# The conditioning matrix's middle part issued from POOL's DMA queue instead of SP's

## The chip, the cores and the metric

The kernel runs on one core of a Trainium2 chip. The metric is the device time of one execution, in microseconds (us). A kernel's time is the median of several executions. The trace comes from one more execution of the same program, taken by the hardware profiler; it has a time of its own, given below.

Engines: PE does matmuls and transposes, DVE and ACT work element by element, POOL and SP here do almost nothing but issue DMAs. A DMA issued by SP goes into SP's hardware queue, one issued by POOL into POOL's software queue; both queues are served by the same 16 DMA engines of the core.

## What is computed

One layer of a decoder trunk, batch 1, 512 tokens, width 2048. Six modulation vectors come from a conditioning vector; they scale, shift and gate the two halves of the layer.

```python
c_act = silu(c)
mod = c_act @ w_mod + b_mod                      # (2048) @ (2048, 12288)
sh1, sc1, g1, sh2, sc2, g2 = split(mod, 6)
h = rms_norm(x, norm_attn) * (1 + sc1) + sh1
qa, ka, va, qb, ckv, qi, ki, wi = split(h @ w_in)
out_a = swa_attention(qa, ka, va, ...)           # window 128, 16 heads
out_b = dsa_attention(qb, ckv, ..., qi, ki, wi)  # 128 keys per query chosen by an indexer, 16 heads
x = x + g1 * (concat(out_a, out_b) @ w_out)
h = rms_norm(x, norm_ffn) * (1 + sc2) + sh2
x = x + g2 * conv_ffn(h, w_up, conv_w, conv_b, w_down)
return rms_norm(x, norm_final)
```

The conditioning matrix w_mod is 2048 x 12288 float32, 100 MB. It is used once, against one vector.

## The kernel before

Float32 precision is kept by splitting every matmul operand in a high part (fp32r, a cast on ACT, line 129) and a low part (a subtraction on DVE, line 130), and by three matmuls per product (`mm3`, lines 134 to 136).

The program is a list of **slots**. A slot is a quarter of a projection unit: 256 KB of weights loaded by `load_raw` (line 123, tag `raw`, 7 buffers), split, and 12 matmuls of 128x512. `drive` walks the slots, loads five ahead and splits three ahead, and calls `step()` after each, which advances the generators that run beside the slots by one piece each. Those are the attention of a pair of heads (`pair_gen`), the preparation of keys and values for the next pair (`prep_gen`), and the conditioning matrix (`mod_gen`).

`mod_gen` goes through groups of 512 columns of w_mod. A group has 16 pieces of 128x512 (256 KB). Each piece is loaded, then multiplied by a column of the conditioning vector and added to `macc` on DVE (lines 181 and 183). After 16 pieces, 16 tiny matmuls (line 193) and one addition (line 230) give the group's columns of `mod`.

The stages, by the profile's time:

- 0 to 180 us: groups 0 to 7 with the keys and the indexer's queries.
- 180 to 390 us: heads of kind A, the indexer's selection (lines 601 to 649), and group 8.
- 390 to 626 us: heads of kind B, eight pairs, four slots a pair, with groups 9 to 13. Their pieces come through `ring_mod` (line 1196) into the ring `mrw` of 5 buffers, and 4 pieces are used per step. Every head also loads a bias tile `tbb` of 256 KB from a DRAM scratch (line 703); its source is a sliding view of one row, in two halves of 64 rows each (`toeplitz`, line 115).
- 626 to 812 us: the output projection `wo`, 64 slots, with groups 14 to 19. Their pieces come through `px_mod` (line 1238) into 8 buffers, 3 used per step. The residual `x` (four tiles of 1 MB, lines 1234 and 1246) is loaded in its first slots and stored again later (line 1265).
- from 812 us: the feed-forward, with groups 20 to 23 in its first part, again through `ring_mod`.

All of these loads are issued by SP, one after the other, in an order that a scheduler sets from priorities when the program is built. An instruction that waits holds back all that stand behind it in SP's order: a load waits for its buffer to be free (mostly for a DVE instruction), and sometimes for an earlier DMA that used the same semaphore. POOL's order is short in this part: three `affine_select` of the indexer (line 609), then nothing until the feed-forward's stores (lines 1064 and 1066).

Of the kernel before, what the change touches and what calls it, by code (L numbers as in the profile page):

```python
# [33 lines left out]
def hybrid_trunk(ctx, tc, xT, cT, wm, bm, nrm, wik, wiq, wi1, sinks, kvn, wuk, wuv, rel, onehot,  # L34
                 wo, wup, cw, cb, wdn, out):
    nc = tc.nc
    act, dve, pe, pool, sp = nc.scalar, nc.vector, nc.tensor, nc.gpsimd, nc.sync
# [80 lines left out]
    ki_ps = bank("acc", "ki_ps")  # L118


    def load_raw(src, name, tag="raw"):
        t = ring.tile([P, 512], F32, tag=tag, bufs=RING[tag], name=name)
        sp.dma_start(t, src)
        return t

    def split(raw, lo, n, name):
# [134 lines left out]
    class Raw:  # L261
# [3 lines left out]
        def load(self, part):  # L265
            if part not in self.t:
                self.t[part] = load_raw(self.src[:, 512 * part:512 * part + 512], f"{self.name}_{part}")
# [66 lines left out]
    with tc.tile_pool(name="ph0", bufs=1) as p0:  # L334
# [13 lines left out]
        def fetch_qi(j):  # L348
            src = wiq[j].rearrange("p a b -> p (a b)")
            for i in range(4):  # L350
                fetched["q", j, i] = load_raw(src[:, 512 * i:512 * i + 512], f"wiq{j}_{i}", "mrw" if i % 2 else "raw")
# [841 lines left out]


    def ring_mod(g, kt):
        return load_raw(wm[g, kt // 4][:, kt % 4], f"mraw{g}_{kt}", "mrw")

    start(ahead(index_gen(), 0))
    start(ahead(keys_gen(), 0))
# [3 lines left out]
    while idle:  # L1203
        step()
    start(mod_gen(range(8, 14), ring_mod, 5, p1, sc_ps, 4), low=True)
    drive(slots, marks["qb0"], marks["wo"])
    env["mh"] = mh = big.tile([P, KT, T], F32R, tag="b2", name="mh")
# [27 lines left out]

    def px_mod(g, kt):
        t = px.tile([P, 512], F32, tag="mraw", bufs=8, name=f"mraw{g}_{kt}")
        sp.dma_start(t, wm[g, kt // 4][:, kt % 4])
        return t

    start(mod_gen(range(14, 20), px_mod, 8, px, o_bank, 3), low=True)
    at = marks["wo"] + 6
    for i in range(1, 4):
# [23 lines left out]
    pdc = tc.tile_pool(name="ph4", bufs=1, reuse_waits="tile")  # L1267
    env["pd"] = pdc.__enter__()
    start(mod_gen(range(20, 24), ring_mod, 5, p2, o_bank, 2), low=True)
    drive(slots, marks["ff"] + 12, marks["join"])  # L1270
    pdc.__exit__(None, None, None)
# [95 lines left out]
```

## Time and profile before

| | |
|---|---|
| time, median of 3 runs | 2227.61 us (2227.18 to 2228.42) |
| time of the profiled execution | 2229.58 us |
| its span, first to last instruction | 2227.8 us |
| PE busy | 2149.5 us, 96% of the span |
| DVE / ACT / POOL busy | 1568.6 / 976.2 / 139.1 us |
| mean granted clock of PE | 0.985 |
| DMA | 367.09 MB, mean 165 GB/s |

The profiled execution lies 1.97 us above the median, and 1.78 us of it lie outside the span. "Busy" of an engine counts its instructions, not its waits. A releaser, shown after an arrow, is what ended an engine's idle time. The chain of waits is followed back from the last instruction, at each step to what released it. The granted clock is the mean of TensorE's two levels, 1.2 and 2.4 GHz, as a share of the upper one.

### The profile page before, as it was taken

Reading aid. Unit: us, or ns where it says so; the run is one execution under the profiler, and the core shown is the slowest. Engines: PE = TensorE matmul, PEld = TensorE weight load, DVE = VectorE, ACT = ScalarE, POOL = GpSimd, SP = SyncE. Lnnn points to the kernel's source line nnn. Section 1 sums busy time; section 2 is a strip of 40 time slices with the busy share of each in tenths; the row PEclk is TensorE's granted clock in tenths of the full one; section 3 lists DMA queues with packets and bytes.
Section 4 is the critical chain, followed back from the end, with each engine's and each line's share of the span. In section 5 each row is a group of like instructions: output and inputs, shape, how many; then the busy total and the mean of one; then the engine's idle time right before and its main releaser. Section 6 shows DMA issues by size and latency. Waiting matters only on the chain.

```text
span 2227.8 us, 30098 instructions
## 1 busy us (share of the span) xinstructions
PE 2149.5 (96%) x10376; PEld 1753.0 (79%) x10376; DVE 1568.6 (70%) x2829; ACT 976.2 (44%) x1850; POOL 139.1 (6%) x184
## 2 busy tenths in 40 slices
PE   7999999779889999999999999999999999999997
PEld 4777777667778888888888888888888888888887
DVE  3888999666679667875757576675757676675666
ACT  5334877556732254333333343333333343333332
POOL 0000000000000000000201011010201010010200
PEclk9999999989999999999999999999999999999998
DMA  9783422556489836743736565563737465563672
GB/s 395 258 292 105 114 72 69 172 172 190 134 301 330 286 99 215 251 150 113 161 101 161 122 135 141 133 149 111 162 98 163 121 136 143 131 150 111 116 256 76
DMA packets 181209, 367.09 MB, mean 165 GB/s; under 512 B 20159, under 2 KB 27343, under 8 KB 174912
## 3 DMA queue, kind: packets, MB, share of 16 engines
q1 hardware_dynamic: 157856, 321.15, 44.2%
q0 software_dynamic: 22336, 42.45, 12.9%
q8 instruction: 81, 1.33, 0.2%
q10 hardware_dynamic: 864, 1.57, 0.2%
q14 instruction: 72, 0.59, 0.1%
HBM read 312.93 MB, written 52.17 MB: 164 GB/s over the span
## 4 chain that ended last, share of the span: by engine, by line
PE 84%; DVE 6%; DMA 6%; ACT 3%; issue 1%; SPq 0%; DVEq 0%; ACTq 0%
PE p L1053 6%; PE p L1055 6%; PE p L1054 6%; DMA mraw<-in_wm_dram 4%; PE qip L134 1%; PE qip L135 1%; PE qip L136 1%; PE o L762 1%; PE tpb L748 1%; DVE macc L183 1%; PE mrow L188 1%; DVE wk L624 1%; DVE top L621 1%; PE mps L193 1%; DVE sa L726 1%
## 5 line engine op out<-in xcount | busy, mean ns | idle before, releaser
L169 ACT CAST dh<-rq 128x512 fp32r<-128x512 f32 x240 | 149.6, 623 | 182.7 <-PE p L1055 143.8
L183 DVE SCALAR_TENSOR_TENSOR macc<-mraw,cact,macc 128x512 f32<-128x512 f32 x240 | 179.7, 749 | 43.5 <-DMA mraw<-in_wm_dram 40.0
L170 DVE TENSOR_TENSOR dl<-rq,dh 128x512 fp32r<-128x512 f32 x240 | 160.9, 685 | 43.1 <-ACT dh L169 42.3
L1054 PE MATMUL p<-dl,ah 128*128 128x512 f32 x480 | 186.7, 389 | 0.0
L1053 PE MATMUL p<-dh,ah 128*128 128x512 f32 x480 | 186.7, 389 | 0.0
L1055 PE MATMUL p<-dh,al 128*128 128x512 f32 x480 | 186.7, 389 | 0.0
L1064 POOL DMA_DIRECT2D cd<-co x72 | 61.4, 852 | 875.1 <-DVE co L1077 873.8
L1054 PEld LDWEIGHTS p<-dl,ah 128*128 128x128 f32 x480 | 90.2, 188 | 18.7
L1053 PEld LDWEIGHTS p<-dh,ah 128*128 128x128 f32 x480 | 90.1, 188 | 18.8
L1055 PEld LDWEIGHTS p<-dh,al 128*128 128x128 f32 x480 | 90.0, 188 | 18.6
L1080 DVE TENSOR_TENSOR v<-p,v 128x512 f32<-128x512 f32 x120 | 82.3, 686 | 6.0 <-PE p L1055 5.2
L1064 POOL DMA_DIRECT2D cd<-v x72 | 61.4, 859 | 128.1 <-DVE v L1082 73.1
L170 DVE TENSOR_TENSOR al<-cu,ah 128x256 fp32r<-128x256 f32 (+2 forms) x60 | 46.7, 779 | 23.8 <-ACT ah L169 21.2
L169 ACT CAST ah<-cu 128x256 fp32r<-128x256 f32 (+2 forms) x60 | 41.5, 692 | 48.1 <-DVE cu L979 25.7
L1077 DVE TENSOR_TENSOR co<-p,v 128x512 f32<-128x512 f32 x80 | 54.9, 686 | 6.7 <-PE p L1055 6.7
L748 PE MATMUL tpb<-identr,sb 128*128 128x128 f32 x160 | 28.8, 316 | 26.0 <-ACT etb L749 26.0
L999 DVE TENSOR_TENSOR rq<-rq,rq 128x512 f32<-128x512 f32 x80 | 52.4, 684 | 0.0
L479 DVE TENSOR_TENSOR qi<-qi,qip 128x512 f32<-128x512 f32 x56 | 38.3, 684 | 14.4 <-PE qip L136 13.6
L748 PEld LDWEIGHTS tpb<-identr,sb 128*128 128x128 f32 x160 | 21.6, 161 | 33.7 <-ACT etb L749 29.6
L1066 POOL DMA_DIRECT2D cd<-co x8 | 4.4, 546 | 668.7 <-DVE co L1077 668.7
L170 DVE TENSOR_TENSOR dl_t<-tw,dh_t 128x512 fp32r<-128x512 f32 x40 | 27.7, 692 | 22.7 <-ACT dh_t L169 22.7
L728 ACT ACTIVATE sb<-sb,nmb 128x512 f32<-128x512 f32 (+2 forms) x64 | 35.3, 553 | 15.6 <-DVE nmb L726 15.3
(4496 smaller groups left out, 6431.2 us busy)
## 6 DMA issues: line engine op xcount, KB each, us to landing
mraw<-in_wm_dram SPq DMA_DIRECT2D x256, 256.0 KB
rq<-in_wdn_dram SPq DMA_DIRECT2D x160, 256.0 KB
mraw<-in_wm_dram SPq DMA_DIRECT2D x32, 1024.0 KB
cd<-co POOLq DMA_DIRECT2D x80, 256.0 KB, 4.5
cd<-v POOLq DMA_DIRECT2D x80, 256.0 KB, 4.7
wiq<-in_wiq_dram SPq DMA_DIRECT2D x32, 256.0 KB
wik<-in_wik_dram SPq DMA_DIRECT2D x8, 592.0 KB
xn<-in_xT_dram SPq DMA_DIRECT2D x4, 1024.0 KB
```

The costliest lines, as they stand in the source:

```text
L169: act.copy(hi_t, full)
L170: dve.tensor_tensor(lo_t, full, hi_t.bitcast(F32), OP.subtract)
L183: dve.scalar_tensor_tensor(acc, t, cact[:, kt:kt + 1], acc, OP.mult, OP.add)
L479: dve.tensor_tensor(qi[i], qi[i], ps, OP.add)
L748: pe.transpose(tp[:, i], self.s[:, c:c + P], ident)
L999: dve.tensor_tensor(self.b[out], self.b[a], self.b[b], OP.add)
L1053: pe.matmul(ps[b], ah[:, tok], wh, start=k == 0, stop=False)
L1054: pe.matmul(ps[b], ah[:, tok], wl, start=False, stop=False)
L1055: pe.matmul(ps[b], al[:, tok], wh, start=False, stop=k == 1)
L1064: pool.dma_start(cd[tb][dq], t, accum_op=OP.add)
L1077: dve.tensor_tensor(t, ps, box["v" if i == 1 else "u", b], OP.subtract)
L1080: dve.tensor_tensor(box["v", b], ps, box["v", b], OP.add)
```

## The change

`load_raw` gets the issuing engine as an argument. Groups 8 to 13 (through `ring_mod`) and groups 14 to 19 (through `px_mod`) are now issued by POOL, 192 loads of 256 KB in all; groups 20 to 23 stay on SP. Buffers, sizes and the arithmetic are as before.

```diff
-    def load_raw(src, name, tag="raw"):
+    def load_raw(src, name, tag="raw", by=sp):
         t = ring.tile([P, 512], F32, tag=tag, bufs=RING[tag], name=name)
-        sp.dma_start(t, src)
+        by.dma_start(t, src)
         return t
...
     def ring_mod(g, kt):
-        return load_raw(wm[g, kt // 4][:, kt % 4], f"mraw{g}_{kt}", "mrw")
+        return load_raw(wm[g, kt // 4][:, kt % 4], f"mraw{g}_{kt}", "mrw", pool if g < 14 else sp)
...
     def px_mod(g, kt):
         t = px.tile([P, 512], F32, tag="mraw", bufs=8, name=f"mraw{g}_{kt}")
-        sp.dma_start(t, wm[g, kt // 4][:, kt % 4])
+        pool.dma_start(t, wm[g, kt // 4][:, kt % 4])
         return t
```

The order of instructions moves as follows. SP, heads of kind B, at the loads of the fourth pair's weights (`qb4r`); `mraw` are pieces of the conditioning matrix, `tbb` the bias tiles, `wukr` weights of the key preparation:

```order
 L123 DMA qb4r_4290<-in_wi_dram 128x512
 L703 DMA tbb_4108<-biasd 128x1x512
-L123 DMA mraw_11_4016<-in_wm_dram 128x512
-L123 DMA mraw_12_4058<-in_wm_dram 128x512
-L123 DMA mraw_13_4061<-in_wm_dram 128x512
 L829 DMA wukr_4208<-in_wuk_dram 128x256
 L703 DMA tbb_4110<-biasd 128x1x512
-L123 DMA mraw_14_4064<-in_wm_dram 128x512
-L123 DMA mraw_15_4067<-in_wm_dram 128x512
-L123 DMA mraw_0_4112<-in_wm_dram 128x512
-L123 DMA mraw_1_4115<-in_wm_dram 128x512
 L123 DMA qb4r_4346<-in_wi_dram 128x512
```

On SP, bias tiles and weights are left, in their old order. POOL, around the indexer's three `affine_select`:

```order
+L123 DMA mraw_3_3860<-in_wm_dram 128x512
+L123 DMA mraw_4_3942<-in_wm_dram 128x512
 L609 AFFINE_SELECT isc_1630<-isc_1630 128x128
 L609 AFFINE_SELECT isc_1631<-isc_1631 128x128
 L609 AFFINE_SELECT isc_1632<-isc_1632 128x128
+L123 DMA mraw_5_3946<-in_wm_dram 128x512
+L123 DMA mraw_6_3949<-in_wm_dram 128x512
```

The fifth piece of group 9 (`mraw_4_3942`, the 21st load of the ring) now stands ahead of the selection in POOL's order, the sixth behind it. Up to the start of the output projection, the orders of PE, DVE and ACT are the same as before. From there on DVE's order changes; its first rows in the output projection (`wo2r` and so on are weights, `x_0` the residual, `macc_0_6151` the sum of group 14):

```order
 L130 TENSOR_TENSOR wo2r_2l<-wo2r_6031,wo2r_2h 128x512
+L181 TENSOR_SCALAR macc_0_6151<-mraw_0_6135,cact 128x512
+L183 SCALAR_TENSOR_TENSOR macc_0_6151<-mraw_1_6137,cact,macc_0_6151 128x512
+L183 SCALAR_TENSOR_TENSOR macc_0_6151<-mraw_2_6139,cact,macc_0_6151 128x512
 L908 SCALAR_TENSOR_TENSOR x_0_6112<-wo0ps,mod,x_0_6112 128x512
+L183 SCALAR_TENSOR_TENSOR macc_0_6151<-mraw_3_6141,cact,macc_0_6151 128x512
 L908 SCALAR_TENSOR_TENSOR x_0_6112<-wo1ps,mod,x_0_6112 128x512
-L181 TENSOR_SCALAR macc_0_6151<-mraw_0_6135,cact 128x512
+L183 SCALAR_TENSOR_TENSOR macc_0_6151<-mraw_4_6143,cact,macc_0_6151 128x512
 L130 TENSOR_TENSOR wo2r_3l<-wo2r_6117,wo2r_3h 128x512
```

The pieces are taken earlier: five stand ahead of the split of `wo2r_3` where one stood. Counted over the whole stage, the old order has 1 to 3 pieces per slot and once 11 (ahead of the split of `wo4r_1`); the new one has 1 to 5 everywhere, and both have used up their 96 pieces by the last slot of `wo11`. The stores of `x` (line 1265) move ahead on SP, from the start of the feed-forward into the loads of `wo6`, `wo10`, `wo14` and later.

## Rows read from the trace of the kernel before

**Rows 1.** The page, parts 1 and 4: PE's busy time; the chain's shares.

```profile
PE 2149.5 (96%) x10376; PEld 1753.0 (79%) x10376; DVE 1568.6 (70%) x2829; ACT 976.2 (44%) x1850; POOL 139.1 (6%) x184
...
PE 84%; DVE 6%; DMA 6%; ACT 3%; issue 1%; SPq 0%; DVEq 0%; ACTq 0%
PE p L1053 6%; PE p L1055 6%; PE p L1054 6%; DMA mraw<-in_wm_dram 4%; PE qip L134 1%; PE qip L135 1%; PE qip L136 1%; PE o L762 1%; PE tpb L748 1%; DVE macc L183 1%; PE mrow L188 1%; DVE wk L624 1%; DVE top L621 1%; PE mps L193 1%; DVE sa L726 1%
```

**Rows 2.** Busy time by stretch: six head pairs of kind B, then the rest.

```profile
core 0: us, PE busy (x) PEld busy (x) DVE busy (x) ACT busy (x) POOL busy (x), PEclk, DMA share, GB/s
396.30:430.50 34.20, 23.28 (x139) 19.20 (x137) 20.57 (x46) 18.02 (x44) 0.00 (x0) 0.85 0.53 168
430.50:464.30 33.80, 25.70 (x150) 20.78 (x150) 21.28 (x44) 17.39 (x42) 0.00 (x0) 0.85 0.58 174
464.30:494.80 30.50, 25.09 (x159) 21.19 (x158) 19.25 (x42) 18.94 (x45) 0.00 (x0) 0.94 0.52 154
494.80:522.40 27.60, 25.83 (x159) 21.04 (x158) 21.55 (x45) 18.52 (x44) 0.00 (x0) 0.94 0.71 214
522.40:552.40 30.00, 26.34 (x159) 21.67 (x158) 19.25 (x42) 18.72 (x45) 0.00 (x0) 0.89 0.56 171
552.40:582.60 30.20, 26.25 (x158) 20.66 (x158) 19.52 (x43) 19.31 (x46) 0.00 (x0) 0.94 0.57 180
582.60:626.00 43.40, 40.75 (x231) 33.48 (x231) 31.95 (x73) 36.57 (x87) 0.00 (x0) 0.92 0.48 147
```

**Rows 3.** The same view: the output projection's two parts, and heads of kind A.

```profile
626.00:752.00 126.00, 119.74 (x562) 96.84 (x562) 108.37 (x171) 32.65 (x56) 0.00 (x0) 0.99 0.94 324
752.00:812.00 60.00, 59.59 (x298) 50.21 (x297) 24.85 (x44) 17.64 (x28) 0.00 (x0) 1.00 0.53 178
240.00:300.00 60.00, 59.25 (x365) 48.04 (x364) 52.73 (x136) 54.41 (x147) 1.28 (x3) 1.00 0.34 95
```

**Rows 4.** Waits, 390 to 626 us: who waited for whom, us, times, longest.

```profile
DVE macc L183 <- DMA mraw<-in_wm_dram: 36.8, 12, 6.0
DVE macc L181 <- DMA mraw<-in_wm_dram: 2.0, 1, 2.0
PE tpb L748 <- ACT etb L749: 26.0, 6, 10.5
SPq L123 <- DVE macc L183: 42.0, 63, 3.8
```

**Rows 5.** SP's timeline: start, us, line, DMA, count.

```profile
472.67 0.51 SPq L703 DMA_DIRECT2D tbb<-biasd  x1
473.28 2.55 SPq L123 DMA_DIRECT2D mraw<-in_wm_dram  x4
```

**Rows 6.** The chain of waits in order of time: start, us, what.

```profile
473.28 9.48 DMA mraw<-in_wm_dram
```

**Rows 7.** DMA from 472 to 484 us in 40 slices: busy tenths, GB/s.

```profile
DMA  2114821295998889968989899998521111111111
GB/s 82 55 41 126 290 96 55 61 137 150 352 280 147 198 307 335 246 212 184 259 280 266 314 348 369 348 314 259 157 82 75 34 55 41 55 55 41 55 55 55
```

**Rows 8.** DMA issues from 396 to 582 us: count, size of one.

```profile
mraw<-in_wm_dram SPq DMA_DIRECT2D x76, 256.0 KB
tbb<-biasd SPq DMA_DIRECT2D x12, 256.0 KB
```

**Rows 9.** DMAs that POOL issues, lines 1066 and 1064: ns min/median/max; landing of L1066's.

```profile
L1066 POOL DMA_DIRECT2D cd<-co x8: 539/542/582, 919.7 to 977.4; - x8
DMA to landing us min/median/max: 2.2/3.0/6.8
...
L1064 POOL DMA_DIRECT2D cd<-v x72: 836/854/1145, 1068.5 to 2113.8; - x72
```

**Rows 10.** Timelines of SP and of POOL at the indexer's selection.

```profile
262.81 0.33 SPq L123 DMA_DIRECT2D mraw<-in_wm_dram  x1
...
290.33 0.29 POOL L609 TENSOR_SCALAR_AFFINE_SELECT isc<-isc 128x128 f32<-128x128 f32 x1 [189.42 <-DVE isc L601]
```

## The prediction

> **What bounds the kernel now.** I read the page first, then busy time by stretch, then the waits of the stretch that stood out, then the DMAs under them.
>
> PE is busy 96% of the span and makes 84% of the chain; the one foreign thing of size on the chain is the landing of `mraw`, pieces of the conditioning matrix, with 4% [rows 1]. Time can only come from where PE idles or runs at a lower clock. The stretches say where: with heads of kind A, PE is busy 59.25 of 60 us at clock 1.00; with heads of kind B the six pairs from 396.3 to 582.6 us take 27.6 to 34.2 us each, for about 25 us of PE work, at clocks from 0.85 to 0.94 [rows 2, 3]. PE idles 10.92 + 8.10 + 5.41 + 1.77 + 3.66 + 3.95 = 33.8 us there. DVE is busy 121 and ACT 111 of these 186 us, so neither is the bound.
>
> The waits name the cause. DVE, which works in order, stands still 36.8 us before line 183 (and 2.0 us before line 181) until a piece of `mraw` has landed, and PE's largest wait, 26.0 us before the transposes of `tpb`, lies behind that through DVE and ACT [rows 4]. The other pieces of matrix work do not wait so.
>
> Why does a piece land late? Take the longest case: SP issues a bias tile `tbb` at 472.67 and the next piece at 473.28, at once when its buffer came free [rows 5]; the piece lands 9.48 us later [rows 6]. The DMA engines are nearly all busy until about 480.5 us, and then for over 3 us only a tenth of them, at some 50 GB/s [rows 7]. The busy share of 0.1 to 0.2 is two engines of sixteen, so about 25 GB/s each: I read this as the bias tile, whose source has an outer dimension of two, going through two engines only, 128 KB each, some 5 us at 25 GB/s. Every piece of `mraw` issued behind it in the same queue has a sixteenth of its bytes behind it on those two engines. So the wait is for place in the queue, not for bandwidth: the DMA share is 0.52 to 0.71 in these pairs [rows 2]. SP's own waits (42.0 us for a buffer at line 123 [rows 4]) also hold back weights, but these are loaded five slots ahead.
>
> **The change, part by part.** *Issue.* 192 loads leave SP and come to POOL. POOL's plain DMAs of the same 256 KB took 0.54 us each [rows 9]; 192 of them are 104 us on an engine that has three instructions between 240 and 812 us. On the path each load costs at most 0.54 in place of the 0.33 us that SP takes [rows 9, 10].
>
> *Landing.* No row shows a load of this size from POOL. The nearest are POOL's plain stores beside the feed-forward's loads: 3.0 us from issue to landing, 2.2 to 6.8 [rows 9]. I take 3.0 for the loads, with 6.8 as the bad end. In the case above: free at 473.2, landed at about 473.2 + 0.54 + 3.0 = 476.8 us, and DVE had come to it at 482.8 - 6.0 = 476.8 us. The wait of 6.0 us would be gone. The ring has 5 buffers, and DVE takes bursts of up to six pieces at about 0.75 us, so the sixth arrives 0.54 + 3.0 us after the first is done, when 5 x 0.75 = 3.75 us have gone: no wait at the median, 3.6 us at the bad end.
>
> *What is late next.* The same two engines stay the tightest. A pair now loads 76/6.2 = 12.3 pieces and two bias tiles [rows 8], and four weight tiles and some 0.5 MB of smaller ones by the code. On each of the two engines that is 2 x 131 + 12.3 x 16.4 + 4 x 16.4 + 33 = 562 KB, or 22.5 us at 25 GB/s, against a PE floor of 24 to 25 us. So they are not the bound, but they have little room, and I leave 1.5 us of PE idle per pair. Bounds: 0 (as with heads of kind A), and 4 us if they run at 20 GB/s (28 us per pair).
>
> *Six pairs.* Idle: 33.8 - 6 x 1.5 = 24.8 us. Clock: busy time times what is missing to 1 gives 3.5 + 3.9 + 1.5 + 1.6 + 2.9 + 1.6 = 14.9 us [rows 2]. The fourth pair, with only 1.77 us idle, still ran at 0.94; if all stayed there, 14.9 - 9.3 = 5.6 us come back; if the pairs came to the clock of the row of heads A, all 14.9. I take 10.
>
> *The last stretch, 582.6 to 626 us.* Idle 2.65 us and 3.3 us of clock; its gap does not come from `mraw`. I take 1 us, of 0 to 5.9.
>
> *Output projection.* PE idles 6.26 us up to 752 us, the DMA share is 0.94 at 324 GB/s [rows 3]. The bytes stay the same, and 2 MB of stores of `x` come in from the feed-forward. 40 slots x 256 KB, 96 pieces, 4 MB of `x` and these stores are 41.7 MB; at 324/0.94 = 345 GB/s they need 121 us, less than the 126 that the part takes. Two full queues would get about 162 GB/s each, and a slot's weights need 256 KB per 2.7 us, 97 GB/s, so weights don't starve. The old order's lump of 11 pieces before one split, behind which PE waited, is gone; the new order asks for five pieces ahead of `wo2r_3`, which must land beside `x`. Between -5 and +6 us; I take a gain of 3.
>
> *POOL's order.* The three selections stand behind the 21st load. SP could issue that load at 262.81 us, and the selection starts at 290.33, when its scores are done [rows 10]: nothing, by 27 us of cover. From the feed-forward on nothing moves but four stores: nothing.
>
> Sum: 24.8 + 10 + 1 + 3 = 38.8 us. From the profiled execution's 2229.58 that is 2190.8; it lies 1.97 us above the median, so 2188.8, say **2189 us**.
>
> **A rule for it.** No row here shows two queues with loads on the same engines. The Trainium skill ("DMA: Bandwidth & Descriptors", section on queues, rings and completion order) states that each DMA engine goes round the queue rows that have work, one packet at a time; by that the pieces pass the bias tile at half rate, and the sum is the one above.
>
> **The rivals.**
>
> *All of it comes back* (0.06): 33.8 + 14.9 + 5.9 + 6.3 = 60.9 us, 2167 us. For it, PE's 98.8% with heads of kind A; against it, the two engines' load.
>
> *The two engines become the bound* (0.13). At 20 GB/s a pair takes 28 us: 6 x 3.05 = 18 us gained, and 4 elsewhere: 2206 us. For it: 562 KB per pair; against: 25 GB/s in [rows 7].
>
> *The change doesn't do what it says* (0.07). If an engine serves descriptors in the order of their issue whatever the queue, a piece still lands behind the bias tile. Then only SP's holds and the evened order count, 3 to 8 us: 2220 to 2225. Against it: POOL's stores landed in 3.0 us with SP's loads running.
>
> *Slower* (0.06): POOL issues too slowly. In the output projection 96 pieces have 126 us, 1.31 us each. Issues longer than that stretch the stage, and as DVE takes pieces in order, the weights' splits behind them, and so PE. The point from which it decides: the pairs gain 36 us, so (126 + 36)/96 = 1.7 us per issue makes the whole slower; at 2.0 us the stage takes 192 us, 66 longer, and the time is 2228 - 36 + 66 = 2258 us. Against it: 0.54 us, 0.85 for the accumulating stores, 1.145 at most [rows 9], with DVE busy beside them. The Trainium skill speaks for it ("SBUF — State Buffer", section on SBUF's two separate sides): a DVE operation that uses both ports locks POOL out of writing descriptors, and an issue of 0.62 us took 3.1 us beside such copies. By that figure, as an estimate, the stage would take 96 x 3.1 = 298 us. The rows of POOL's issues here don't agree with it: DVE's work in this kernel is nearly all subtractions and multiply-adds with two inputs.
>
> **How the numbers follow.** The forecast (2172 to 2202 us) has 0.68, all back 0.06, two engines 0.13, no effect 0.07, slower 0.06. The range from 2165 to 2212 takes in the first three, 0.87. A measurement of this kernel can tell 0.2%, 4.5 us, from no change: faster means under 2223. Of the no-effect case 0.04 lies under it and 0.03 above: faster 0.91, same 0.03, slower 0.06.
>
> **What would show it.** DVE's wait for `mraw` between 390 and 626 us falls from 38.8 us to under 10. The six pairs take about 25 us each, at clocks near 1, with a DMA share near 0.7. POOL's issues at lines 123 and 1238 take about 0.55 us. The part of the output projection with pieces takes 120 to 126 us. Nothing changes after it. It would be wrong if pieces from POOL land later than 5 us after issue, if PE finds another wait of 4 us per pair (bias tiles or weights late on SP), or if POOL's issues take over 1.3 us.

## The result and the profile after

| | before | after |
|---|---|---|
| time, median | 2227.39 us (2223.52 to 2228.42, 4 runs) | 2207.74 us (2204.59 to 2213.56, 4 runs) |
| ratio | | 0.9918, 95% interval 0.9893 to 0.9943 |
| the profiled execution: time, span | 2229.58, 2227.8 us | 2213.56, 2211.8 us |
| six head pairs, first to last | 186.3 us | 161.3 us |
| output projection, first matmul of `wo0` to that of `wo11` | 151.0 us | 155.8 us |

The kernel became 19.65 us faster by the medians; the forecast was 38.6. The profiled execution of after is the slowest of its four, 5.8 us above the median, so its stretches add up to less than the medians differ by (2229.58 - 2213.56 = 16.0 us).

By stretch, the first six cut at the same matmuls as the pairs of [rows 2]. The last three are cut only near those of [rows 2, 3] (PE executes 259 instructions in the seventh, 231 in before), so their lengths aren't compared here. The columns are stretch, its length, busy time of PE, PE's weight loads, DVE, ACT and POOL (instructions in brackets), granted clock, DMA share and GB/s.

```profile
400.80:427.20 26.40, 23.03 (x139) 19.34 (x138) 19.95 (x46) 17.95 (x44) 5.90 (x11) 0.94 0.63 212
427.20:453.70 26.50, 24.40 (x150) 19.92 (x150) 21.31 (x44) 17.30 (x42) 8.59 (x16) 0.94 0.63 199
453.70:478.40 24.70, 23.81 (x160) 19.82 (x158) 18.72 (x41) 18.65 (x44) 5.36 (x11) 1.00 0.64 204
478.40:504.00 25.60, 24.18 (x158) 19.73 (x158) 20.80 (x45) 18.32 (x43) 8.04 (x15) 1.00 0.72 224
504.00:531.20 27.20, 24.05 (x159) 19.71 (x158) 19.78 (x44) 18.37 (x44) 5.93 (x12) 1.00 0.61 196
531.20:562.10 30.90, 27.65 (x160) 21.73 (x158) 19.72 (x47) 19.57 (x46) 4.25 (x8) 0.89 0.60 192
562.10:607.00 44.90, 41.62 (x259) 33.95 (x260) 31.74 (x73) 37.79 (x89) 1.60 (x3) 0.96 0.53 166
607.00:736.00 129.00, 120.20 (x539) 97.82 (x536) 109.55 (x174) 31.45 (x53) 49.30 (x92) 0.95 0.93 331
736.00:796.00 60.00, 59.66 (x295) 50.22 (x293) 23.08 (x38) 17.74 (x28) 0.00 (x0) 1.00 0.38 125
```

The six pairs, the first six lines, gain 186.3 - 161.3 = 25.0 us. PE's idle time in them falls from 33.8 to 14.2 us (length minus PE busy, summed) and its busy time from 152.5 to 147.1, as the clock is higher. The first pair begins at 400.8 us instead of 396.3, so 4.5 us are lost ahead of it, and from `wo0` to `wo11` the output projection takes 155.8 us instead of 151.0. The pairs gain what was to be gained only in part (25.0 of 34.8 us), and two places that were costed at nothing or better cost time.

The waits from 390 us to the end of heads of kind B (607 us), with us in total, times and the longest:

```profile
POOL mraw L1238 <- DVE nmb L726: 53.7, 2, 27.7
DVE macc L183 <- DMA mraw<-in_wm_dram: 19.4, 17, 3.0
PE tpb L748 <- ACT etb L749: 9.1, 6, 3.4
```

DVE waits for pieces of the conditioning matrix 19.4 us instead of 38.8 [rows 4], in 17 waits of at most 3.0 us; PE's wait behind it falls from 26.0 to 9.1. POOL's 53.7 us are harmless: it waits for memory that the heads still hold, with nothing else to do.

POOL's part in the page of after, groups of instructions (busy us, mean ns | idle before) and DMA issues (KB each, median us to landing):

```profile
L123 POOL DMA_DIRECT2D mraw<-in_wm_dram x96 | 51.6, 538 | 357.6 <-DVE macc L181 131.1
L1238 POOL DMA_DIRECT2D mraw<-in_wm_dram x96 | 51.4, 536 | 133.4 <-DVE nmb L726 53.7
mraw<-in_wm_dram POOLq DMA_DIRECT2D x192, 256.0 KB, 5.6
```

An issue costs the 0.54 us of [rows 9]. A landing costs 5.6 us, not the 3.0 that I had taken from POOL's stores. The profile counts a landing from the start of the instruction that issues it, so the 0.54 us are part of the 5.6.

The chain of waits of after around one late piece (start us, us, what), and the timeline of SP at that place:

```profile
429.05 7.96 DMA mraw<-in_wm_dram
437.01 0.03 issue
437.03 0.02 DVEq L183
437.06 0.04 issue
437.10 0.75 DVE macc L183
```

```profile
427.53 0.51 SPq L703 DMA_DIRECT2D tbb<-biasd  x1
```

This is the case of [rows 5, 6] again, with the piece now in another queue. SP issues a bias tile at 427.53, POOL a piece at 429.05, and the piece takes 7.96 us where it took 9.48. DVE stands still for it once more, for 1.6 us instead of 6.0.

### The profile page after: what moved, and what is told of

Read it like the earlier page. It is cut to its first block, busy times and chain, and to the rows that moved or that the text cites. A ratio compares the mean times of both kernels' runs of the same rounds, so it can differ in the third digit from the quotient of the medians.

```text
span 2211.8 us, 30173 instructions
## 1 busy us (share of the span) xinstructions
PE 2149.8 (97%) x10376; PEld 1752.7 (79%) x10376; DVE 1567.8 (71%) x2829; ACT 975.8 (44%) x1850; POOL 242.2 (11%) x376
## 4 chain that ended last, share of the span: by engine, by line
PE 72%; issue 17%; DMA 5%; POOL 2%; DVE 2%; ACT 1%; SPq 0%; POOLq 0%; DVEq 0%; ACTq 0%
PE p L1053 6%; PE p L1055 6%; PE p L1054 6%; DMA mraw<-in_wm_dram 4%; POOL mraw L1238 1%; POOL mraw L123 1%; PE qip L134 1%; PE mrow L188 1%; PE qip L135 1%; PE qip L136 1%; DMA xn<-in_xT_dram 0%; DVE macc L183 0%; PE mps L193 0%; DMA wiq<-in_wiq_dram 0%; PE cT L1105 0%
## 5 line engine op out<-in xcount | busy, mean ns | idle before, releaser
L183 DVE SCALAR_TENSOR_TENSOR macc<-mraw,cact,macc 128x512 f32<-128x512 f32 x240 | 179.6, 748 | 26.2 <-DMA mraw<-in_wm_dram 22.5
L123 POOL DMA_DIRECT2D mraw<-in_wm_dram x96 | 51.6, 538 | 357.6 <-DVE macc L181 131.1
L1238 POOL DMA_DIRECT2D mraw<-in_wm_dram x96 | 51.4, 536 | 133.4 <-DVE nmb L726 53.7
L169 ACT CAST ah<-cu 128x256 fp32r<-128x256 f32 (+2 forms) x60 | 41.5, 692 | 49.4 <-DVE cu L979 25.9
L728 ACT ACTIVATE sb<-sb,nmb 128x512 f32<-128x512 f32 (+2 forms) x64 | 35.3, 552 | 13.3 <-DVE nmb L726 13.0
L378 DVE SCALAR_TENSOR_TENSOR macc<-mraw,cact,macc 128x512 f32<-128x512 f32 x54 | 40.3, 746 | 0.4
```

The source lines that it names most:

```text
L123: by.dma_start(t, src)
L169: act.copy(hi_t, full)
L183: dve.scalar_tensor_tensor(acc, t, cact[:, kt:kt + 1], acc, OP.mult, OP.add)
L1238: pool.dma_start(t, wm[g, kt // 4][:, kt % 4])
```

## The experiments

All eight are edits of the kernel before or after, each timed beside the kernel before on the same chip: e1 to e4 on one chip, e5 to e9 on another. The wait is DVE's for pieces of `mraw` (lines 181 and 183), from 390 us to the first matmul of the output projection; the pairs are the six of [rows 2]. The kernel before had medians of 2227.39, 2227.12 and 2226.62 us beside them.

| kernel | groups 8 to 13 | groups 14 to 19 | bias tile: engines, queue | DVE's wait, us | pairs, us | time, us | ratio (95%) |
|---|---|---|---|---|---|---|---|
| before | SP | SP | 2, SP | 38.4 | 186.3 | 2227 | 1 |
| after | POOL | POOL | 2, SP | 16.9 | 161.3 | 2207.74 | 0.9918 (0.9893 to 0.9943) |
| e1_ring_only | POOL | SP | 2, SP | 16.7 | 159.5 | 2201.22 | 0.9885 (0.9864 to 0.9907) |
| e2_px_only | SP | POOL | 2, SP | 38.8 | 185.6 | 2231.21 | 1.0016 (1.0004 to 1.0028) |
| e5_bias_by_pool | SP | SP | 2, POOL | 16.3 | 159.1 | 2204.29 | 0.9896 (0.9878 to 0.9913) |
| e9_bias4 | SP | SP | 4, SP | 18.5 | 163.8 | 2202.86 | 0.9891 (0.9876 to 0.9906) |
| e3_bias16 | SP | SP | 16, SP | 4.6 | 144.8 | 2187.14 | 0.9817 (0.9798 to 0.9837) |
| e7_bias16_ring | POOL | SP | 16, SP | 10.8 | 149.1 | 2192.49 | 0.9841 (0.9824 to 0.9857) |
| e8_bias16_px | SP | POOL | 16, SP | 5.6 | 145.7 | 2192.69 | 0.9841 (0.9823 to 0.986) |
| e4_bias16_pool | POOL | POOL | 16, SP | 11.0 | 149.6 | 2195.66 | 0.9856 (0.9835 to 0.9878) |

The theory after the result: pieces were late for their place behind the bias tiles in SP's queue; POOL's queue takes them out of that place, but they share the tile's two engines still, and land later than I had put in. The main rivals: SP's own waits for buffers hold the pieces (then the bias tiles don't matter), or engines serve in order of issue whatever the queue (then POOL's queue doesn't matter).

### Each half of the change alone

**e1_ring_only** leaves groups 14 to 19 on SP:

```diff
-        pool.dma_start(t, wm[g, kt // 4][:, kt % 4])
+        sp.dma_start(t, wm[g, kt // 4][:, kt % 4])
```

> The change for groups 8 to 13 alone (pieces of the ring issued by POOL); groups 14 to 19 stay on SP, and the orders of PE, DVE and ACT are those of the kernel before. Theory (the changed kernel gained 25 us in the head pairs and gave back some 5 us in the output projection because DVE's order and the residual's loads changed there): the pairs keep 24 to 27 us of gain, the output projection takes 151 us as before, and the time is 2200 to 2205 us. Rival (the loss in the output projection comes from the pairs ending earlier, whatever issues groups 14 to 19): the output projection takes 155 us or more, and the time is 2206 to 2210 us.

**e2_px_only** leaves groups 8 to 13 on SP:

```diff
-        return load_raw(wm[g, kt // 4][:, kt % 4], f"mraw{g}_{kt}", "mrw", pool if g < 14 else sp)
+        return load_raw(wm[g, kt // 4][:, kt % 4], f"mraw{g}_{kt}", "mrw")
```

> The change for groups 14 to 19 alone; groups 8 to 13 stay on SP, with the orders of PE, DVE and ACT of the changed kernel. Theory: no gain in the pairs (DVE waits 35 us or more for pieces), 3 to 6 us lost in the output projection: 2229 to 2234 us. Rival (the output projection is served as well from POOL, and its loss in the changed kernel has another cause): 2222 to 2228 us.

Measured: 2201.22 and 2231.21 us, both inside their theory's range. The whole gain, 25.9 us, is in the ring of groups 8 to 13; groups 14 to 19 on POOL cost 4.1 us by themselves, and the full change lies 6.5 us above the half. The same sign stands in both pairs with 16 engines: e8 above e3 by 5.5, e4 above e7 by 3.2 us, though there the intervals overlap.

Where e2 loses its time is not what was expected. In its trace the output projection takes 150.3 us from `wo0` to `wo11`, no more than the 151.0 of before, and not 3 to 6 us more; what that execution is behind, it loses ahead of the pairs, where the clock fell (see below). So the price of groups 14 to 19 shows in the medians, but its place isn't shown by e2.

### The bias tiles spread over the engines

**e3_bias16** is the kernel before, all pieces on SP. The scratch that the bias tiles are read from holds 16 shifted copies of each row instead of 2, so the outer dimension of a tile's source is 16:

```diff
-    biasd = dram.tile([32, 2, 1024], F32, name="biasd")
+    biasd = dram.tile([32, 16, 1024], F32, name="biasd")
...
-        return bass.AP(tensor=biasd.tensor, offset=biasd.offset + 2048 * (HEADS * g + head) + 384 * g + P - 1,
-                       ap=[[1024 - 64, 2], [-1, 64], [1, n]])
+        return bass.AP(tensor=biasd.tensor, offset=biasd.offset + 16384 * (HEADS * g + head) + 384 * g + P - 1,
+                       ap=[[1024 - 8, 16], [-1, 8], [1, n]])
...
-                for k in range(2):
+                for k in range(16):
```

> All loads on SP, as in the kernel before; only the bias tiles' source is laid out in 16 shifted copies in place of 2 (its outer dimension is 16 in place of 2), so that a tile should go through 16 DMA engines in place of two. The orders of PE, DVE, ACT and SP are those before. Theory (pieces landed late because they stood behind a bias tile on two engines): DVE's wait for pieces between 390 and 626 us falls from 38.8 us to under 15, PE gets 20 us or more back there, 2198 to 2208 us. Rival (SP's order holds the pieces back, or the landing is late for all loads): the wait stays at 30 us or more, and the time is 2222 to 2230 us.

**e4_bias16_pool** is the same edit on the kernel after.

> The changed kernel with the bias tiles' source in 16 copies, as in the run with that alone. Theory (POOL's pieces still land in 5.3 us at the median because bias tiles fill two engines): landing falls to 3 to 4 us, DVE's wait for pieces from 19 us to under 8, the pairs gain 6 to 10 us more, 2196 to 2202 us. Rival (5.3 us is what a load from POOL takes here): landing stays above 5 us, and the time is that of the changed kernel, 2204 to 2210 us.

Measured: 2187.14 and 2195.66 us. e3 gains 40.0 us without moving a load to another queue, about the forecast's sum for the change under study and 11 us more than the best that its theory allowed; its wait of 4.6 us lies far under the 15. In e4 neither side had it right: pieces land in 4.7 us, not in 3 to 4 and not above 5, and the wait is 11.0 us, not under 8, while the time is at the edge of the theory's range. The waits of e3 from 390 to 555 us:

```profile
PE tpb L748 <- ACT etb L749: 3.0, 5, 1.9
DVE macc L183 <- DMA mraw<-in_wm_dram: 4.6, 8, 1.3
```

and its DMA issues from 396 to 560 us (count, KB, median us to landing), then the shortest, median and longest landing of a piece from 396 to 541 us:

```profile
mraw<-in_wm_dram SPq DMA_DIRECT2D x74, 256.0 KB, 4.5
tbb<-biasd SPq DMA_DIRECT2D x14, 256.0 KB, 4.0
...
DMA to landing us min/median/max: 3.1/4.5/5.8
```

A bias tile now lands in 4.0 us, and a piece in 4.5, at most 5.8. SP still waits 37.5 us for `macc` in that window, against 38.5 in before from 390 us to its first matmul of the output projection: SP's waits for buffers are not what made the pieces late. That rival falls, and the two engines of the bias tile stand as the cause. The Trainium skill states the rule behind it ("DMA: Bandwidth & Descriptors", section "Why a DMA increments its semaphore by 16 and not by 1"): a copy is split over as many engines as the largest number up to 16 that divides the slowest dimensions of its two sides. The traces agree: with 2 in the outer dimension a piece behind the tile took 9.48 us, with 16 no piece of that window took more than 5.8.

One path of the delay isn't told apart. In before SP also stood still until earlier loads had landed:

```profile
SPq L123 <- DMA mraw<-in_wm_dram: 25.0, 8, 5.6
SPq L123 <- DMA tbb<-biasd: 7.2, 3, 3.0
SPq L829 <- DMA tbb<-biasd: 6.3, 2, 3.2
```

These 38.5 us come from the late landings, and in e3 1.5 us are left of them. No run shows how much of DVE's wait went through them and how much through the place on the two engines; both go with the tile's two engines.

In e3 the six pairs run at clock 1.00; three of their lines:

```profile
419.70:443.20 23.50, 23.12 (x150) 18.68 (x150) 21.19 (x44) 17.23 (x42) 0.00 (x0) 1.00 0.70 218
443.20:467.20 24.00, 23.80 (x159) 19.82 (x158) 18.91 (x41) 18.65 (x44) 0.00 (x0) 1.00 0.71 217
467.20:491.90 24.70, 24.40 (x159) 19.70 (x158) 21.49 (x47) 18.21 (x44) 0.00 (x0) 1.00 0.79 242
```

With POOL on top (e4), 8.5 us of the gain are lost again.

**e9_bias4** takes 4 copies instead of 16:

```diff
+    biasd = dram.tile([32, 4, 1024], F32, name="biasd")
...
+        return bass.AP(tensor=biasd.tensor, offset=biasd.offset + 4096 * (HEADS * g + head) + 384 * g + P - 1,
+                       ap=[[1024 - 32, 4], [-1, 32], [1, n]])
...
+                for k in range(4):
```

> All pieces on SP as before, the source of the bias tiles in 4 shifted copies instead of 2 (or 16), so that a tile goes through 4 DMA engines. Theory of the queue: a tile's landing halves from 9.48 us to about 5 us, the pieces behind it land some 4 us earlier, DVE's waits for pieces in the six pairs are 10 to 20 us (38.8 with two, 4.6 with sixteen) and the time is 2190 to 2207. Rival, a threshold: the pieces are late only while a tile takes longer than the ring of five hides, so 4 engines give all that 16 give, 2185 to 2190.

Measured: a wait of 18.5 us and 2202.86 us. That is between 2 and 16 engines, in the upper part of what the theory of the queue gave; there is no threshold by which four would do. With 2, 4 and 16 engines the wait is 38.4, 18.5 and 4.6 us. The trace doesn't name a packet's engine; that the number of engines is what counts is read from this row. (The 9.48 us that this expectation and that of e5 give to the tile are the landing of the piece behind it; how long the tile itself took with two or four engines, the traces don't tell.) Four engines instead of two gain about what POOL's queue gains (24 us against 26 in e1).

### The tiles moved instead of the pieces

**e5_bias_by_pool** is the kernel before with the bias tiles, still through two engines, issued by POOL:

```diff
-            sp.dma_start(self.tb[:, :self.nt], self.tb_src)
+            pool.dma_start(self.tb[:, :self.nt], self.tb_src)
```

> The kernel before, with one line changed: the two bias tiles of a head (tba, tbb, still through two DMA engines each) are issued by POOL, and every piece of the conditioning matrix stays on SP; the orders of PE, DVE and ACT are those of before. Theory of the place in the queue: a piece that SP issues is no longer behind a bias tile of its own queue, so it lands in 3.5 to 5 us, DVE's waits for pieces in the six pairs fall from 38.8 us to under 10, and the time is 2188 to 2205 (PE may wait for a tile where POOL's landing is later than SP's 9.48 us). Rival, the two engines: fourteen sixteenths of a piece go through free engines but the piece is complete only when its share in the two loaded engines is through, whatever queue asked for it, so the waits stay over 20 us and the time is 2208 to 2225.

Measured: 2204.29 us, inside the range of the theory of the place, but with a wait of 16.3 us where it said under 10. It hardly matters which of the two leaves SP's queue: the time is that of e1 within the intervals, and the wait is 16.3 us against 16.7. What is left is shown by the issues of e5 from 396 to 560 us:

```profile
mraw<-in_wm_dram SPq DMA_DIRECT2D x77, 256.0 KB, 5.6
tbb<-biasd POOLq DMA_DIRECT2D x13, 256.0 KB, 11.3
```

Pieces from SP take 5.6 us here too, against 4.5 with the tile spread. I read this so: in two queues a piece no longer waits for the whole tile, but it shares its two engines with it. So both rivals hold in part. Taking the tile out of the pieces' queue removes the larger part of DVE's wait (38.4 to 16.3 us), and spreading it removes a rest that a second queue can't (16.3 to 4.6). The tile's 11.3 us can't be put down to the sharing alone: POOL also cuts it into other packets (7474 under 512 B in this window, 1670 in before), and its landing from SP in before isn't in the trace.

### POOL's own price

**e7_bias16_ring** is e3 with groups 8 to 13 on POOL, **e8_bias16_px** e3 with groups 14 to 19 on POOL; with e3 and e4 they make a square. The one line of each:

```diff
+        return load_raw(wm[g, kt // 4][:, kt % 4], f"mraw{g}_{kt}", "mrw", pool if g < 14 else sp)
```

```diff
+        pool.dma_start(t, wm[g, kt // 4][:, kt % 4])
```

> Groups 8 to 13 of the conditioning matrix are issued by POOL, groups 14 to 19 by SP, and the bias tiles go through 16 DMA engines as in the best kernel so far (2187.1 us, which has all of this on SP). The orders of PE, DVE and ACT are the same as there. Theory: POOL's load takes its 5.3 us to land by itself, so DVE's waits for pieces are about 11 us in the six pairs against 4.6, and the time is 2188 to 2193. Rival: the 5.3 us come from the bias tiles' two engines, and with 16 engines POOL's pieces land in about 3.6 us; waits under 6 us, time 2184 to 2188.

> Groups 14 to 19 of the conditioning matrix are issued by POOL, groups 8 to 13 by SP, and the bias tiles go through 16 DMA engines. With the kernels that have both parts on SP (2187.1), both on POOL (2195.7) and the ring alone on POOL, this makes a square of four. Theory: the price of the second part on POOL is its own and has nothing to do with the bias tiles: 2190 to 2194, that is 3 to 7 us above both on SP; the clock falls again near 211 us, as in the three kernels so far with this part on POOL, although nothing of it has run by then. Rival: the price of both parts is one of the two sharing POOL's queue: then this kernel is at 2186 to 2189, and no fall of the clock near 211 us would say that the fall is a matter of the execution.

Measured: 2192.49 us with a wait of 10.8, and 2192.69 with a wait of 5.6. The issues of e7 from 396 to 560 us:

```profile
mraw<-in_wm_dram POOLq DMA_DIRECT2D x74, 256.0 KB, 4.6
tbb<-biasd SPq DMA_DIRECT2D x14, 256.0 KB, 4.2
```

A median landing of 4.6 us is neither the 5.3 of the theory nor the 3.6 of the rival, and it is what SP's pieces take in e3 (4.5). So the median isn't POOL's own: the bias tile's two engines add 0.9 (5.5 in after, over the same window). Still, POOL's wait is 6.2 us longer than SP's and the pairs 4.3 us longer, and e4 against e8 says the same (3.9 us). Two things differ in the traces. The longest landing is 7.3 us in e7 and 5.8 in e3. And POOL issues back to back every 0.79 us, as here in after:

```profile
429.05 0.54 POOL L123 DMA_DIRECT2D mraw<-in_wm_dram  x1 [0.25 <-DVE denb L738]
429.84 0.54 POOL L123 DMA_DIRECT2D mraw<-in_wm_dram  x1 [0.25 <-DVE macc L183]
```

SP does it every 0.64 us (in before at 489.19 and 489.83), and DVE takes a piece about every 0.78 us in its bursts (three in 2.33 us, at 428.79 in after). That these two make the 6.2 us wasn't tested. The ratios of e7 and e3 differ by 0.0024, with intervals that overlap; the pairs and the waits carry the reading more than the times do.

The price of groups 14 to 19 on POOL shows without any bias tile in two engines too (e8 above e3), as the theory had it; the intervals of these two overlap, so it is likely and not shown.

## Why the prediction was right and wrong

**The cause, right.** The bias tiles ahead of them make the pieces late (e3), and a second queue takes them out of that place (e1, e5). The case "no effect" falls by the same runs, and "slower" by the issue of 0.54 us.

**The landing, mis-sized.** This is the term that failed. I took 3.0 us from POOL's 16 plain stores beside the feed-forward, a stretch with less traffic, and kept 6.8 as the bad end; it was 5.5. By the prediction's own reckoning, the sixth piece of a burst is needed 3.75 us after the first buffer comes free. (The reckoning counts the issue twice: a landing is counted from the start of the issue, so 0.54 doesn't come on top, neither here nor in the 476.8 us of the case.) A landing of 5.5 leaves a wait of 5.5 - 3.75 = 1.8 us a burst where I had none; measured were 17 waits of up to 3.0. With 4.5 us, in e3, it would leave 0.8, and the eight waits measured there are at most 1.3. The trace of before gives no landing for any load of this stretch. But it has POOL's 144 accumulating stores of the same size, of which I had used the time to issue and not the landing:

```profile
L1064 POOL DMA_DIRECT2D cd<-v x72: 836/854/1145, 1068.5 to 2113.8; - x72
DMA to landing us min/median/max: 3.8/4.7/12.3
```

The prediction said that it would be wrong if pieces landed later than 5 us after issue, and so it came.

**Where the rest went.** Of the 38.8 us summed up, the profiled execution has 16.0. The six pairs are 9.8 us short (25.0 of 34.8), the output projection 7.8 (-4.8 in place of +3), and 4.5 were lost ahead of the pairs, where nothing was put in.

**The six pairs.** Idle was to fall by 24.8 us and fell by 33.8 - 14.2 = 19.6; busy time was to fall by 10 with the clock and fell by 5.4. Both are short for one reason, the waits that stayed: with nearly all of them gone in e3, idle is 3.8 us, the clock 1.00, and busy time falls by 152.5 - 141.0 = 11.5. So the 10 us for the clock was right in size, but not a term of its own; it comes with the idle time and not before.

**The rate.** Time follows DVE's wait through the kernels of the table: 40.0 us for 38.4 - 4.6 = 33.8 us of wait from before to e3, 1.2 us for each, 25.9 for 21.7 in e1 and 22.3 for 22.1 in e5. A forecast that had put 17 us of wait in place of under 10 would have said about 2202 us (2227 - 1.2 x 21), and the rest of the way to 2207.7 is about what groups 14 to 19 cost on POOL.

**Two engines become the bound.** This rival gave 2206 us, next to the result, and half of its mechanism was there. It had the two engines short of throughput, with 28 us for every pair. The pairs took 24.7 to 30.9 at a DMA share near 0.6. What the engines did was to delay the pieces that met a tile: with the tiles spread (e7 against e1) the pairs take 149.1 instead of 159.5 us.

**Output projection, wrong.** A gain of 3 us was forecast, of -5 to +6; in the profiled execution it lost 4.8 (155.8 against 151.0 us for `wo0` to `wo11`). The stretch falls into two: the first line below is before from `wo0` to `wo4`, the second after, the third and fourth the same from `wo4` to `wo8`.

```profile
596.80:661.10 64.30, 61.41 (x338) 50.26 (x339) 52.15 (x94) 32.81 (x71) 0.00 (x0) 0.95 0.74 250
```

```profile
576.20:648.60 72.40, 64.19 (x339) 51.58 (x340) 56.58 (x100) 33.99 (x74) 14.85 (x28) 0.91 0.80 286
```

```profile
661.10:712.80 51.70, 48.23 (x209) 38.39 (x208) 46.30 (x72) 12.04 (x20) 0.00 (x0) 0.97 0.94 324
```

```profile
648.60:694.30 45.70, 45.70 (x210) 37.68 (x209) 43.33 (x69) 12.51 (x21) 21.88 (x42) 1.00 0.97 334
```

The later part lost its lump of 11 pieces and gains 6.0 us, as forecast: PE doesn't idle at all there. The end of the stage, `wo8` to `wo11`, takes 37.7 us at clock 0.95 instead of 35.0 at 1.00 (35.3 in e8). The earlier part loses 8.1: pieces and `x` are asked for together, and these waits stand there in after (the same places have 2.8 and 4.2 us in before):

```profile
PE mps L193 <- DVE macc L183: 5.5, 1, 5.5
DVE x L908 <- DMA x<-in_xT_dram: 5.4, 1, 5.4
```

The first tiny matmuls of group 14 now stand behind 165 matmuls of the projection instead of 185, and DVE's sums, behind `x`, don't come earlier to the same degree. e8 has the same picture against e3 (70.9 and 64.7 us in the earlier part, 45.7 and 49.8 in the later), so it belongs to the move of groups 14 to 19: the earlier part loses, the later part gains, and the sum is small. That the loss comes from the order, and not from the added traffic, is read from the trace and wasn't tested. The sizes differ from run to run: for `wo0` to `wo11`, groups 14 to 19 on POOL against SP, the four pairs of kernels give -0.7 (e2 and before), +1.5 (e4 and e7), +2.4 (e8 and e3) and +6.2 us (after and e1).

**Ahead of the pairs, nothing: half right.** The profiled execution of after loses 4.5 us there, where no instruction that PE, DVE or ACT executes stands elsewhere. Busy time from 0 to 28 us and from 214 to 218 us shows where, before first and after second:

```profile
0.00:28.00 28.00, 18.31 (x106) 8.32 (x106) 6.42 (x18) 14.66 (x25) 3.89 (x16) 1.00 0.94 377
214.00:218.00 4.00, 4.00 (x26) 3.57 (x26) 3.96 (x11) 2.40 (x6) 0.00 (x0) 1.00 0.48 133
```

```profile
0.00:28.00 28.00, 18.56 (x90) 7.04 (x90) 5.51 (x14) 13.06 (x22) 3.89 (x16) 0.94 0.95 377
214.00:218.00 4.00, 4.00 (x15) 3.26 (x15) 3.22 (x9) 0.75 (x2) 0.91 (x2) 0.62 0.55 146
```

It is the clock. After the first four experiments I took it for a price of groups 14 to 19 on POOL, since exactly the kernels with these had the fall near 214 us. e8 has them and kept 1.00 there; e5 and e7, without them, fell to 0.69 and 0.63. Of the ten profiled executions five fall and five don't, with PE's idle time ahead of it the same to 0.1 us in before and e2 (1.16 and 1.18 us). The low clock from 0 to 28 us stands in e7 too (0.94) and not in e1 (1.00), which moves the same groups. So I read it as a matter of the execution; no kernel was profiled twice to show it. That selections behind loads in POOL's order cost nothing, as predicted, stands by e1 (first matmul of `qb0` at 356.5 us, 356.4 in before).

**From the feed-forward on, nothing: right.** From its first matmul to the first of the last projection it takes 1351.8 us in both.

## What to carry to other kernels

Late loads behind a slow one are first a question of the slow one: ask how many DMA engines it goes through, before moving the others to another queue. Here the spread over 16 engines was worth 40 us, the second queue for the ring 26, and the spread with both parts of the change 31, less than the spread alone. Where a landing time is missing, take it from all transfers of the same size that the trace has, not from the quickest few, and set it against the time that the ring's buffers cover: here 3.75 us, so that 3.0 meant no wait and 4.7 a wait in every burst.

## What was not expected of the hardware

- Two queues give a piece its turn on a busy engine but not a free way: at the median 4.5 us with the tile spread, 5.5 from POOL beside a tile of two engines; in the two single cases shown, 7.96 in another queue than the tile and 9.48 behind it in one queue.
- The Trainium skill says ("DMA: Bandwidth & Descriptors", section "Issuing engines are not separate DMA queues") that issuing from several engines saves only the time of the issue. The time here says more: e1 gains 25.9 us with issues that are longer on POOL (0.54 us) than on SP (0.33), because a piece in another queue no longer stands behind the tile; e5, with the pieces on SP and only the tile's issue moved, gains 22.3.
- TensorE's clock fell from its upper to its lower level near 214 us in five of the ten profiled executions, after the same 1.2 us of idle time. Over the stretch from 198 to 356 us those five take 1.5 to 3.3 us longer than before (first matmul of `qa0` to that of `qb0`), so a single profile can't tell such a loss from one of the change.
